# Two projections with the same weights as one: the high and low part of x side by side in a two-layer decoder trunk

## The chip, the cores and the metric

One core of a Trainium2 chip runs the whole program. The metric is the device time of one execution in microseconds (us), the median of the runs; lower is better. TensorE (PE) multiplies, ScalarE (ACT) and VectorE (DVE) do the elementwise work, SyncE (SP) issues the DMAs. TensorE writes its sums to PSUM, a small memory of eight banks of 128 partitions x 512 float32.

## What is computed

The reference takes 256 tokens of width 2048 through two layers. Cut to what matters here:

```python
def _even_layer(x, w_in, ...):
    hproj = x @ w_in                                  # 2048 -> 7704 columns
    (qa, kc, vc, ks, vs, kw, vw, ga, gate_a, qb, kb, vb, gate_b) = _split(hproj, EVEN_SIZES)
    o_a = _nsa(...) * jax.nn.silu(gate_a)             # sparse attention, 8 heads
    o_b = _stick_breaking(...) * jax.nn.silu(gate_b)  # 8 heads
    y = jnp.concatenate([o_a, o_b], axis=-1) @ w_out
    return _layer_norm(DEEPNORM_ALPHA * x + y, ln_g, ln_b)

def _odd_layer(x, w_in, ...):
    q, k, v, gate = _split(x @ w_in, ODD_SIZES)       # 2048 -> 8192 columns
    o = _diff_attn(q, k, v, ...) * jax.nn.silu(gate)  # 8 heads
    return _layer_norm(DEEPNORM_ALPHA * x + o @ w_out, ln_g, ln_b)
```

All of it is float32. Most of the arithmetic is the four big products with weight matrices.

## The kernel before

**Products in parts.** Every float32 operand of a big product is split into a high and a low part (`split`, L125: ACT casts the source to the high part, DVE subtracts it from the source to get the low one). A product a x b is then three matmuls: high x high, high x low, low x high, summed in PSUM.

**Two kinds of projection.** In the first kind, `xs_group` and `xs_apart`, tokens are stationary and 390 or 512 weight columns move (L202 to L204). In the second, `ws_block` (L176), 128 weight columns are stationary and the 256 tokens move, so that the result comes out transposed, [128 columns, 256 tokens]. A block covers the 2048 inputs in 16 steps k of 128, with three matmuls of 256 moving columns in each: weights high x tokens high (L181), weights high x tokens low (L182), weights low x tokens high (L183). `ws_pair` (L185) runs two blocks, one into each half of one PSUM bank, and hands the bank to the consumer. The query, key and gate columns of both layers go this way: kc, kr, qa, qb, kb, gate in the even layer, q and k in the odd one.

**Weights.** `load_split` brings a block's weights by one DMA (1 MB) to a tile `wr` (3 buffers) and splits it in two halves, each to a tile `wh` (high) and `wl` (low), 4 buffers each; a half holds 8 of the 16 steps.

**Moving operand.** `new_lhs` (L245) gives the tokens' high parts in four tiles and the low parts in four more; `lhs_of` picks the slice of step k. These tiles are xT (input), oT and oT1 (attention outputs), yT (the normalised rows between the layers).

**Attention.** Attention is written as generators. `tick` (L167) advances up to two of them after each block, so attention work of TensorE lies between and inside the projection blocks. The consumers of a pair are `rope` (DVE, four instructions), scaled copies (ACT) or `silu` (ACT and DVE).

**Order.** A scheduler orders the instructions of each engine when the program is built, by priorities (the program order) and its own estimates; buffers of a pool come free when their last reader is done. On the chip each engine takes its instructions in that order, each waiting for its semaphores. Names used below: `ss` are attention scores in PSUM, `sm` the softmax rows made of them, `pT` transposed probabilities in PSUM and `pk` their parts, `pcT` the same of the compressed branch, `aT` and `po` those of the odd layer's attention and its output, `yt` the transposes that become yT.

Of the kernel before, what the change touches and what calls it, by code (L numbers as in the profile page):

```python
# [10 lines left out]
F32 = mybir.dt.float32  # L11
F32R = mybir.dt.float32r
# [20 lines left out]
# columns of ev_w_in: q kc vc ks vs kw vw gates gate_a qb kb vb gate_b  # L33
# [3 lines left out]
# stationary-weight column blocks of the even layer, in the order they are used  # L37
# [3 lines left out]
# packed constants: name -> (offset, width)  # L41
# [42 lines left out]
def hybrid_trunk(ctx: ExitStack, tc: tile.TileContext, a):  # L84
# [10 lines left out]
    # the one table set with all of Exp, Ln, Abs, Square, Copy and Identity  # L95
# [21 lines left out]
    # ---- zeros through the tensor engine while the first loads are under way, so that its clock is up  # L117
# [6 lines left out]
    # ---- splitting float32 into two parts of 12 bits each, exactly  # L124
# [4 lines left out]
    def mm3(o, lhs, rhs, start, stop):  # L129
        """o += lhs.T @ rhs, both in parts"""  # L130
        (ah, al), (bh, bl) = lhs, rhs
        nc.tensor.matmul(o, ah, bh, start=start, stop=False, skip_group_check=True)
        nc.tensor.matmul(o, ah, bl, start=False, stop=False, skip_group_check=True)
        nc.tensor.matmul(o, al, bh, start=False, stop=stop, skip_group_check=True)

    # ---- weights: one DMA per tile, then the two parts
# [9 lines left out]
    def load_split(src, n, alloc=part, pieces=None, m=1):  # L146
        """pieces(j): called before each part of a half, which is then loaded and split by itself"""
        raw = raw_tile(n)
        if not pieces:
            nc.sync.dma_start(raw, src)  # L150
        out = []
        for s in range(2):
            h, l = alloc("wh", n // 2), alloc("wl", n // 2)
            w = n // 2 // m
            for j in range(m):
                d = slice((m * s + j) * w, (m * s + j + 1) * w)
                if pieces:
                    pieces(m * s + j)
                    nc.sync.dma_start(raw[:, d], src[:, d])
                split(h[:, j * w:(j + 1) * w], l[:, j * w:(j + 1) * w], raw[:, d])  # L160
            out.append((h, l))
        return out

    # work in stages, one stage of each after every block of a projection
# [11 lines left out]
    def ws_block(src, ps, xh, xl):  # L176
        """ps[cols, tokens] = W[:, 128 cols].T @ x.T"""
        parts = load_split(src.rearrange("p k c -> p (k c)"), 2048)
        for k in range(NK):
            h, l = (t.rearrange("p (k c) -> p k c", c=P)[:, k % 8, :] for t in parts[k // 8])  # L180
            nc.tensor.matmul(ps, h, xh(k), start=(k == 0), stop=False)  # L181
            nc.tensor.matmul(ps, h, xl(k), start=False, stop=False)  # L182
            nc.tensor.matmul(ps, l, xh(k), start=False, stop=(k == NK - 1))  # L183

    def ws_pair(src, i, name, xh, xl):  # L185
        ps = acc(name)
        for c in range(2):
            ws_block(src[i + c], ps[:, c * SEQ:(c + 1) * SEQ], xh, xl)
            tick()
        return ps.rearrange("p (c t) -> p c t", c=2)  # L190
# [4 lines left out]
    def xs_mm(o, t, parts, half, k0, w, xh, xl, start, stop, c0=0):  # L195
        """o[tokens of t, cols] += x[:, two k] @ W[two k, cols]"""
        h, l = (p.rearrange("p (k c) -> p k c", c=w) for p in parts[half])
        s = slice(t * P, (t + 1) * P)
        cs = slice(c0, c0 + o.shape[1])
        for j in range(2):  # L200
            k = k0 + 2 * half + j
            nc.tensor.matmul(o, xh(k)[:, s], h[:, j, cs], start=(start and j == 0), stop=False)  # L202
            nc.tensor.matmul(o, xh(k)[:, s], l[:, j, cs], start=False, stop=False)  # L203
            nc.tensor.matmul(o, xl(k)[:, s], h[:, j, cs], start=False, stop=(stop and j == 1))  # L204

    def xs_group(src, w, name, xh, xl, ahead=None):
        """ps[t][tokens, cols] = x @ W[:, w cols]"""
        ps = [acc(f"{name}{t}") for t in range(NT)]
        for kc in range(4):
            m = 2 if ahead and kc < 1 else 1  # L210
            parts = xs_parts(src, w, kc, part, ahead and (lambda j: ahead(kc, j * 2 // m, 2 // m)), m)
            order = [(half, t) for half in range(2) for t in range(NT)]
            if not ahead:
                order.sort(key=lambda z: z[1])
            for half, t in order:
                xs_mm(ps[t][:, :w], t, parts, half, 4 * kc, w, xh, xl, kc + half == 0, kc + half == 4)
            tick()
        return ps

    def xs_apart(src, name, xh, xl, in_units, orders, ready, n_last=1, m=1):  # L220
        """like xs_group, one token tile after the other, the weights kept; ready(t, c0, ps) after each"""
# [14 lines left out]
    # ---- constants  # L236
# [7 lines left out]
    # ---- x transposed, in parts  # L244
    def new_lhs(name):  # L245
        return ([unit(f"{name}h{i}", [4, SEQ], F32R) for i in range(4)],
                [unit(f"{name}l{i}", [4, SEQ], F32R) for i in range(4)])

    def lhs_of(parts):
        return [lambda k, t=t: t[k // 4][:, k % 4, :] for t in parts]  # L250

    xT = new_lhs("xT")
    xh, xl = lhs_of(xT)

    xraw = [unit("xraw", [4, SEQ]) for _ in range(4)]

    def load_x(i, k, n):
        xr = xraw[i][:, k:k + n]
        nc.sync.dma_start(xr, a["xT"][:, 4 * i + k:4 * i + k + n, :])
        split(xT[0][i][:, k:k + n], xT[1][i][:, k:k + n], xr)  # L260
# [15 lines left out]
    def load_constants():  # L276
        nc.sync.dma_start(cst, a["cst"])
        nc.sync.dma_start(sml, a["sml"])
        # lambda = exp(lq1.lk1) - exp(lq2.lk2) + lambda_init, negated, on every partition
# [11 lines left out]
    # ---- helpers  # L291
    def rope(ps, cos, sin, out):
        """ps, out: [128 d, 2, 256 tokens]"""
# [8 lines left out]
    def log_sigmoid_parts(g, w, tag):  # L302
        """e = ln(1 + exp(-|g|))"""
# [18 lines left out]
    def rsqrt(out, v, n, name):  # L322
        """out = v ** -0.5, one Newton step after exp(-ln(v) / 2)"""
# [9 lines left out]
    def softmax_rows(ps, n, mask, name):  # L333
        """ps: [128 q, 2, n] negated scaled scores -> unnormalised p and 1/sum for both."""
# [11 lines left out]
    def transposed(p, t, ps):  # L346
        """p: [128 q, (t+1)*128 keys] of query tile t into ps[keys, 3*128]: k0 t0 | k0 t1 | k1 t1"""
# [4 lines left out]
    def add_pv(o, v, pT, start, stop):  # L352
        """o[d, 256 q] += v.T @ p.T over both key tiles"""
# [3 lines left out]
    # =========================== even layer ===========================  # L357
    ws, xs = a["ev_ws"], a["ev_xs"]
    # token-major columns: gates | vs | vw | vb
# [25 lines left out]
    kvT = unit("kvT", [2, 2, SEQ])  # compressed-branch k, v: [d, (k v), head, token]  # L385
    for i in range(2):
        ps = ws_pair(ws, 2 * i, f"kc{i}", xh, xl)
        nc.scalar.copy(kvT[:, i], ps)
    kr = [unit(f"kr{i}", [2, 2, SEQ], F32R) for i in range(2)]  # roped keys: [d, head, (select window), token]
    for i in range(2):  # L390
        ps = ws_pair(ws, 4 + 2 * i, f"kr{i}", xh, xl)
# [4 lines left out]
    # compression MLPs  # L396
    kcmpT = cpool.tile([P, 2, NCMP], F32, name="kcmpT")
    # compressed values: their three products of parts in one pass, the parts at rows 0, 32 and 64
# [64 lines left out]
    # native sparse attention, two heads at a time  # L463
# [3 lines left out]
    def held(i):  # L467
        """for the attention of heads 2i and 2i+1 of all 16"""
# [4 lines left out]
    def nsa_proj(i):  # L473
        ps = ws_pair(ws, 8 + 2 * i, f"qa{i}", xh, xl)
# [8 lines left out]
    def nsa_attn(i, qc, qs):  # L483
# [3 lines left out]
        # compressed branch  # L487
# [20 lines left out]
        # selected and window branches  # L508
# [32 lines left out]
        pk0 = [unit(f"pk0{j}", [2, 2, SEQ], F32R) for j in range(2)]  # [key, (select window), head, query]  # L541
# [19 lines left out]
    def sb_proj(i):  # L561
        ps = ws_pair(ws, 16 + 2 * i, f"qb{i}", xh, xl)
        qb = wk("qc", [2, SEQ])
        nc.scalar.activation(qb, ps, AF.Copy, scale=SCALE)
        ps = ws_pair(ws, 24 + 2 * i, f"kb{i}", xh, xl)
# [49 lines left out]
    def gate_pair(i):  # L615
        """o = attention * silu(gate), in parts, for heads 2i and 2i+1 of all 16"""
        ps = ws_pair(ws, 32 + 2 * i, f"gate{i}", xh, xl)
        s = silu(ps.rearrange("p c t -> p (c t)"), 512)
        sl = slice(2 * (i % 2), 2 * (i % 2) + 2)
        nc.vector.tensor_mul(s, s, held(i).rearrange("p c t -> p (c t)"))  # L620
        split(oT[0][i // 2][:, sl].rearrange("p c t -> p (c t)"), oT[1][i // 2][:, sl].rearrange("p c t -> p (c t)"), s)
# [16 lines left out]
    def cols(halves, c):  # L638
        """columns c * 512 ... of a row of 2048 kept in two units"""
        return halves[c // 2][:, c % 2 * 512:(c % 2 + 1) * 512]  # L640

    # ---- output projection, residual and layer norm
# [9 lines left out]
    def out_layer(wout, lhs, resid, name, finish, g=None, n_last=1):  # L652
        """resid[t] = alpha * resid[t] + lhs @ wout (times g), then finish(t, its mean and 1 / deviation)"""
# [47 lines left out]
    def normalise(t, scale, bias):  # L701
        """resid[t] becomes the normalised row, its scaled and shifted transpose goes to yT"""
# [5 lines left out]
        for c in range(4):  # L708
# [8 lines left out]
            split(yT[0][c][:, :, ts], yT[1][c][:, :, ts], y)  # L717
# [4 lines left out]
    # =========================== odd layer ===========================  # L722
    yh, yl = lhs_of(yT)
    ws, xs = a["od_ws"], a["od_xs"]
# [20 lines left out]
    def diff_proj(h):  # L745
        ps = ws_pair(ws, 4 * h, f"q{h}", yh, yl)
        q = wk("qr", [2, SEQ])
        rope(ps, C("cosq"), C("sinq"), q)
        ps = ws_pair(ws, 4 * h + 2, f"k{h}", yh, yl)
# [66 lines left out]
    def gate_out(g, sg):  # L816
        yield
        for j in range(2):
# [5 lines left out]
            for b in range(2):  # L824
                c = 2 * j + b
                gs = gn1[:, 4 * g + c:4 * g + c + 1]
                nc.scalar.activation(oT[0][g][:, c], pt[:, b], AF.Copy, scale=gs)
                nc.vector.scalar_tensor_tensor(oT[1][g][:, c], pt[:, b], gs, oT[0][g][:, c].bitcast(F32),
# [8 lines left out]
    def store(t, scale, bias):  # L837
        """resid[t] is r * g: r * g * scale + (g * bias + b)"""
# [28 lines left out]
def _layout(x, ev_w_in, ev_pe_k, ev_pe_v, ev_w1_k, ev_w2_k, ev_w1_v, ev_w2_v, ev_w_out, ev_ln_g, ev_ln_b,  # L867
# [3 lines left out]
    def grouped(w, width):  # L871
        """[2048, n * width] -> [n, 128, 16, width]"""
# [54 lines left out]
```

## Time and profile before

| | us |
|---|---|
| median of 3 runs (977.92 to 978.41) | 978.25 |
| span of the profiled execution, first to last instruction | 976.2 |
| TensorE matmul busy | 966.6 |
| TensorE weight load busy | 891.6 |
| VectorE busy | 668.7 |
| ScalarE busy | 505.6 |

The profiled execution's own time is not listed apart from the three runs; its span lies 2.05 us under their median. Busy time is the union of an engine's instructions; matmuls overlap in it, since each is shown from its start to its modelled end while the next has begun. How densely TensorE works is therefore read from the distance between the starts of neighbouring matmuls, the pitch, and not from the length of one.

### The profile page before, as it was taken

What the parts mean: (1) busy time and instruction counts of PE and PEld (TensorE: products, weight loads), DVE (VectorE), ACT (ScalarE), POOL (GpSimd) and SP (SyncE); (2) the same over time, 40 slices, a digit from 0 to 9 for tenths busy, and PEclk for the clock granted to TensorE, in tenths of its full rate; (3) what the DMA queues carried; (4) which work ended last, traced back from release to release, by engine and by line L of the source; (5) the groups of instructions that cost most, each with busy time, mean ns of one, the idle gap of its engine ahead of it and who ended that gap; (6) DMA issues with size and microseconds to landing.
All of it is one profiled execution on the core that took longest, in us unless ns stands there. A gap on an engine that the chain in (4) does not pass through costs nothing.

```text
span 976.2 us, 15916 instructions
## 1 busy us (share of the span) xinstructions
PE 966.6 (99%) x6497; PEld 891.6 (91%) x6497; DVE 668.7 (69%) x1107; ACT 505.6 (52%) x812; POOL 1.2 (0%) x8
## 2 busy tenths in 40 slices
PE   8999999999999999999999999999999999999998
PEld 6999999999999999988888889999999988888886
DVE  6544577695766856666598556777778776667676
ACT  5544444475657856535473443455545556664340
POOL 0000000000000000000000000000000000000000
PEclk9999999999999999999999999999999999999999
DMA  8765546643334345756547555544544445557542
GB/s 306 256 207 195 186 169 249 257 138 121 136 123 141 130 174 177 277 193 229 180 150 266 207 176 178 189 156 170 173 167 154 160 168 177 191 193 258 194 151 87
DMA packets 30457, 180.80 MB, mean 185 GB/s; under 512 B 3504, under 2 KB 5296, under 8 KB 11952
## 3 DMA queue, kind: packets, MB, share of 16 engines
q1 hardware_dynamic: 30384, 179.79, 52.3%
q8 instruction: 51, 0.84, 0.3%
q14 instruction: 22, 0.18, 0.1%
HBM read 177.68 MB, written 2.10 MB: 184 GB/s over the span
## 4 chain that ended last, share of the span: by engine, by line
PE 96%; DMA 1%; DVE 1%; ACT 1%; SPq 0%; issue 0%; DVEq 0%; ACTq 0%
PE k L182 3%; PE k L183 3%; PE k L181 3%; PE gate L183 3%; PE q L182 3%; PE gate L182 3%; PE gate L181 3%; PE q L181 3%; PE q L183 3%; PE oo L204 3%; PE oo L202 3%; PE oo L203 3%; PE odv L203 3%; PE odg L202 3%; PE odv L202 3%; PE odg L203 3%
## 5 line engine op out<-in xcount | busy, mean ns | idle before, releaser
L127 DVE TENSOR_TENSOR wl<-wr,wh 128x1024 fp32r<-128x1024 f32 (+3 forms) x330 | 383.2, 1166 | 225.1 <-ACT wh L126 217.9
L126 ACT CAST wh<-wr 128x1024 fp32r<-128x1024 f32 (+3 forms) x330 | 329.7, 1003 | 349.6 <-PE eo L204 40.9
L181 PE MATMUL q<-yTh,wh 128*128 128x256 f32 x256 | 72.9, 285 | 0.0
L181 PE MATMUL gate<-xTh,wh 128*128 128x256 f32 x256 | 72.8, 284 | 0.0
L183 PE MATMUL gate<-xTh,wl 128*128 128x256 f32 x256 | 72.5, 283 | 0.0
L181 PE MATMUL k<-yTh,wh 128*128 128x256 f32 x256 | 72.4, 283 | 0.0
L182 PE MATMUL k<-yTl,wh 128*128 128x256 f32 x256 | 72.4, 283 | 0.0
L183 PE MATMUL k<-yTh,wl 128*128 128x256 f32 x256 | 72.4, 283 | 0.0
L182 PE MATMUL gate<-xTl,wh 128*128 128x256 f32 x256 | 72.4, 283 | 0.0
L183 PE MATMUL q<-yTh,wl 128*128 128x256 f32 x256 | 72.4, 283 | 0.0
L182 PE MATMUL q<-yTl,wh 128*128 128x256 f32 x256 | 72.4, 283 | 0.0
L204 PE MATMUL oo<-wh,oT1l 128*128 128x512 f32 (+1 forms) x144 | 52.7, 366 | 0.0
L203 PE MATMUL oo<-wl,oT1h 128*128 128x512 f32 (+1 forms) x144 | 52.7, 366 | 0.0
L202 PE MATMUL oo<-wh,oT1h 128*128 128x512 f32 (+1 forms) x144 | 52.7, 366 | 0.0
L202 PE MATMUL odg<-wh,yTh 128*128 128x512 f32 x128 | 50.3, 393 | 0.0
L202 PE MATMUL odv<-wh,yTh 128*128 128x512 f32 x128 | 50.1, 392 | 0.0
L202 PE MATMUL eo<-wh,oTh 128*128 128x512 f32 x128 | 50.0, 391 | 0.0
L203 PE MATMUL odv<-wl,yTh 128*128 128x512 f32 x128 | 50.0, 390 | 0.0
L204 PE MATMUL odv<-wh,yTl 128*128 128x512 f32 x128 | 49.9, 390 | 0.0
L203 PE MATMUL eo<-wl,oTh 128*128 128x512 f32 x128 | 49.9, 390 | 0.0
L204 PE MATMUL odg<-wh,yTl 128*128 128x512 f32 x128 | 49.9, 390 | 0.0
L203 PE MATMUL odg<-wl,yTh 128*128 128x512 f32 x128 | 49.8, 389 | 0.0
(287 smaller groups left out, 2494.0 us busy)
## 6 DMA issues: line engine op xcount, KB each, us to landing
wr<-in_ev_ws_dram SPq DMA_DIRECT2D x48, 1024.0 KB, 4.8
wr<-in_od_xs_dram SPq DMA_DIRECT2D x32, 1024.0 KB, 4.8
wr<-in_od_ws_dram SPq DMA_DIRECT2D x32, 1024.0 KB, 4.9
wr<-in_ev_wo_dram SPq DMA_DIRECT2D x16, 1024.0 KB, 4.8
wr<-in_od_wo_dram SPq DMA_DIRECT2D x16, 1024.0 KB, 4.9
wr<-in_ev_xs_dram SPq DMA_DIRECT2D x12, 780.0 KB, 4.6
w<-in_w_dram SPq DMA_DIRECT2D x8, 512.0 KB, 8.4
wr<-in_ev_xs_dram SPq DMA_DIRECT2D x6, 390.0 KB, 6.7
```

The costliest lines, as they stand in the source:

```text
L126: nc.scalar.copy(h, src)
L127: nc.vector.tensor_sub(l, src, h.bitcast(F32))
L181: nc.tensor.matmul(ps, h, xh(k), start=(k == 0), stop=False)
L182: nc.tensor.matmul(ps, h, xl(k), start=False, stop=False)
L183: nc.tensor.matmul(ps, l, xh(k), start=False, stop=(k == NK - 1))
L202: nc.tensor.matmul(o, xh(k)[:, s], h[:, j, cs], start=(start and j == 0), stop=False)
L203: nc.tensor.matmul(o, xh(k)[:, s], l[:, j, cs], start=False, stop=False)
L204: nc.tensor.matmul(o, xl(k)[:, s], h[:, j, cs], start=False, stop=(stop and j == 1))
```

## The change

The tokens' high and low parts now lie side by side: `new_lhs` gives eight tiles of two steps each, and in each step 256 columns of the high part are followed by 256 of the low part. `ws_block` issues one matmul of 512 moving columns with the high weights, into a whole PSUM bank, and one of 256 with the low weights, onto its first half. So each block has a bank of its own, and the two halves have to be added: ACT copies the second half to a tile `wsum`, DVE adds the first half to it. The consumers read `wsum` in place of PSUM. The products in `xs_group` and `xs_apart` are as before, on slices of the new tiles. Where a split writes four steps, as for yT, it is now two splits of two steps. Comments and docstrings are dropped.

```diff
-    def ws_block(src, ps, xh, xl):
+    def ws_block(src, ps, xx):
         parts = load_split(src.rearrange("p k c -> p (k c)"), 2048)
         for k in range(NK):
             h, l = (t.rearrange("p (k c) -> p k c", c=P)[:, k % 8, :] for t in parts[k // 8])
-            nc.tensor.matmul(ps, h, xh(k), start=(k == 0), stop=False)
-            nc.tensor.matmul(ps, h, xl(k), start=False, stop=False)
-            nc.tensor.matmul(ps, l, xh(k), start=False, stop=(k == NK - 1))
-
-    def ws_pair(src, i, name, xh, xl):
-        ps = acc(name)
+            nc.tensor.matmul(ps, h, xx(k), start=(k == 0), stop=False, skip_group_check=True)
+            nc.tensor.matmul(ps[:, :SEQ], l, xx(k)[:, :SEQ], start=False, stop=(k == NK - 1), skip_group_check=True)
+
+    def ws_pair(src, i, name, xx):
+        out = wk("wsum", [2, SEQ])
         for c in range(2):
-            ws_block(src[i + c], ps[:, c * SEQ:(c + 1) * SEQ], xh, xl)
+            ps = acc(f"{name}{c}")
+            ws_block(src[i + c], ps, xx)
+            nc.scalar.copy(out[:, c], ps[:, SEQ:])
+            nc.vector.tensor_add(out[:, c], out[:, c], ps[:, :SEQ])
             tick()
-        return ps.rearrange("p (c t) -> p c t", c=2)
+        return out
...
     def new_lhs(name):
-        return ([unit(f"{name}h{i}", [4, SEQ], F32R) for i in range(4)],
-                [unit(f"{name}l{i}", [4, SEQ], F32R) for i in range(4)])
+        return [unit(f"{name}{i}", [2, 2, SEQ], F32R) for i in range(8)]
 
     def lhs_of(parts):
-        return [lambda k, t=t: t[k // 4][:, k % 4, :] for t in parts]
+        return [lambda k, j=j: parts[k // 2][:, k % 2, j, :] for j in range(2)]
+
+    def both_of(parts):
+        return lambda k: parts[k // 2][:, k % 2].rearrange("p j t -> p (j t)")
+
+    def two(parts, j, i):
+        return parts[i][:, :, j, :]
...
-            split(yT[0][c][:, :, ts], yT[1][c][:, :, ts], y)
+            for j in range(2):
+                split(two(yT, 0, 2 * c + j)[:, :, ts], two(yT, 1, 2 * c + j)[:, :, ts], y[:, 2 * j:2 * j + 2])
```

**TensorE, odd layer, key projection of head 1**, the end of its first block and the start of its second. Before (`k1` is the pair's PSUM bank, `yTh3`, `yTl3` the high and low tokens of the last four steps):

```order
L181 MATMUL k1_6333<-yTh3_4609,wh_6340 128x256
L182 MATMUL k1_6333<-yTl3_4613,wh_6340 128x256
L183 MATMUL k1_6333<-yTh3_4609,wl_6341 128x256
L181 MATMUL k1_6333<-yTh0_4606,wh_6394 128x256
L182 MATMUL k1_6333<-yTl0_4610,wh_6394 128x256
L183 MATMUL k1_6333<-yTh0_4606,wl_6395 128x256
```

Now, with a bank for each block (`k10`, `k11`):

```order
L181 MATMUL k10_5648<-yT7_3989,wh_5655 128x512
L182 MATMUL k10_5648<-yT7_3989,wl_5656 128x256
L181 MATMUL k11_5693<-yT0_3982,wh_5696 128x512
L182 MATMUL k11_5693<-yT0_3982,wl_5697 128x256
L181 MATMUL k11_5693<-yT1_3983,wh_5696 128x512
```

Three instructions of 256 columns have become one of 512 and one of 256; what stands next to them has not moved.

**ScalarE, odd layer, around the end of head 1's key projection.** Before (`wh` are casts of weight halves, the numbers rise with the program; L795 squares the attention output for its mean):

```order
L126 CAST wh_6558<-wr_6556 128x1024
L126 CAST wh_6562<-wr_6556 128x1024
L126 CAST aTs0_6454<-aT_6450 128x384
L126 CAST wh_6654<-wr_6652 128x1024
L126 CAST q1_6468<-qr_6326 128x256
L126 CAST wh_6658<-wr_6652 128x1024
```

Now:

```order
L190 COPY wsum_5647<-k10_5648 128x256
L126 CAST wh_5834<-wr_5832 128x1024
L126 CAST wh_5838<-wr_5832 128x1024
L190 COPY wsum_5647<-k11_5693 128x256
L126 CAST aTs0_5742<-aT_5738 128x384
L126 CAST wh_5917<-wr_5915 128x1024
L126 CAST wh_5921<-wr_5915 128x1024
L126 CAST ks_5753<-qc_5746 128x512
```

A copy of each block's second half stands between the casts: that of block k10 ahead of wh_5834, which belongs to the second block after k11, and that of k11 two casts later.

**VectorE, even layer, where the attention of three head pairs meets** (L338, after the change L352, named ISA, makes softmax rows `sm` of scores `ss`). Before, from the low parts of block kb1's weights on:

```order
L127 TENSOR_TENSOR wl_2489<-wr_2486,wh_2488 128x1024
L127 TENSOR_TENSOR wl_2493<-wr_2486,wh_2492 128x1024
L127 TENSOR_TENSOR pk01_2134<-pT0_2345,pk00_2133 128x2x256
L127 TENSOR_TENSOR pk11_2136<-pT1_2346,pk10_2135 128x2x128
L127 TENSOR_TENSOR pcT_1241<-tcmp_2357,pcT_1241 15x512
L127 TENSOR_TENSOR pk01_2366<-pT0_2369,pk00_2365 128x2x256
L127 TENSOR_TENSOR pk11_2368<-pT1_2370,pk10_2367 128x2x128
L338 ISA sm_2385,smst_2386<-ss_2381,cst_86 128x128
L338 ISA smst_2386 128x1
L338 ISA sm_2385,smst_2386<-ss_2381,cst_86 128x128
L338 ISA smst_2386 128x1
L338 ISA sm_2399,smst_2400<-ss_2395,cst_86 128x256
```

Now, up to the low part of the second weight half of block qb11:

```order
L127 TENSOR_TENSOR pcT_1137<-tcmp_2084,pcT_1137 15x512
L127 TENSOR_TENSOR pk01_2093<-pT0_2096,pk00_2092 128x2x256
L127 TENSOR_TENSOR pk11_2095<-pT1_2097,pk10_2094 128x2x128
L352 ISA sm_2112,smst_2113<-ss_2108,cst_86 128x128
L352 ISA smst_2113 128x1
L352 ISA sm_2112,smst_2113<-ss_2108,cst_86 128x128
L352 ISA smst_2113 128x1
L352 ISA sm_2126,smst_2127<-ss_2122,cst_86 128x256
L352 ISA smst_2127 128x1
L352 ISA sm_2126,smst_2127<-ss_2122,cst_86 128x256
L352 ISA smst_2127 128x1
L127 TENSOR_TENSOR wl_2144<-wr_2137,wh_2143 128x1024
```

Before, the weights of the next pair were split ahead of this attention work, which lies in the second block of qb1; now the second half of that same block's weights is split behind it. On TensorE, 2 matmuls of block qb11 and 10 of an attention output (`po`) stand between the scores ss_2122 and the first matmul that reads wl_2144.

## Rows read from the trace of the kernel before

**Rows 1.** The page: busy time of each engine, share of the span, instructions.
```profile
PE 966.6 (99%) x6497; PEld 891.6 (91%) x6497; DVE 668.7 (69%) x1107; ACT 505.6 (52%) x812; POOL 1.2 (0%) x8
```
**Rows 2.** The page: chain of work that ended last, shares by engine.
```profile
PE 96%; DMA 1%; DVE 1%; ACT 1%; SPq 0%; issue 0%; DVEq 0%; ACTq 0%
```
**Rows 3.** Waits of TensorE: total us, times, longest us.
```profile
PE ev L202 <- ACT wh L126: 2.0, 2, 1.2
...
PE cmp L425 <- DMA w<-in_w_dram: 0.7, 1, 0.7
```
**Rows 4.** Timeline, TensorE, odd layer: start us, length us, instruction; 256 columns.
```profile
604.60 0.28 PE L183 MATMUL k<-yTh,wl 128*128 128x256 f32 x1
...
606.04 0.28 PE L183 MATMUL q<-yTh,wl 128*128 128x256 f32 x1
```
**Rows 5.** Timeline, TensorE, odd layer, product with 512 moving columns.
```profile
549.64 0.39 PE L203 MATMUL odv<-wl,yTh 128*128 128x512 f32 x1
...
553.04 0.39 PE L203 MATMUL odv<-wl,yTh 128*128 128x512 f32 x1
```
**Rows 6.** Timeline, TensorE, attention output, where 512 and 256 columns alternate.
```profile
238.55 0.40 PE L134 MATMUL po<-pk,vsw 128*128 128x512 f32 x1
238.79 0.28 PE L132 MATMUL po<-pk,vsw 128*128 128x256 f32 x1
...
239.02 0.28 PE L134 MATMUL po<-pk,vsw 128*128 128x256 f32 x1
239.14 0.40 PE L132 MATMUL po<-pk,vsw 128*128 128x512 f32 x1
```
**Rows 7.** The page: DMA issues, count, KB each, us to landing.
```profile
wr<-in_ev_ws_dram SPq DMA_DIRECT2D x48, 1024.0 KB, 4.8
...
wr<-in_od_ws_dram SPq DMA_DIRECT2D x32, 1024.0 KB, 4.9
```
**Rows 8.** Groups by line and shape: busy us, mean ns, idle before.
```profile
L126 ACT CAST wh<-wr 128x1024 fp32r<-128x1024 f32 x280 | 293.1, 1049 | 316.5 <-PE q L182 40.1 <-PE k L182 36.1 <-PE odv L204 29.5
...
L126 ACT CAST q<-qr 128x256 fp32r<-128x256 f32 x8 | 3.2, 402 | 0.0
...
L126 ACT CAST pk<-pT 128x256 fp32r<-128x256 f32 x8 | 3.0, 374 | 0.9 <-PE pT L528 0.9
...
L127 DVE TENSOR_TENSOR wl<-wr,wh 128x1024 fp32r<-128x1024 f32 x280 | 341.5, 1224 | 200.0 <-ACT wh L126 193.7 <-PE pT L527 1.7
...
L127 DVE TENSOR_TENSOR yTl<-yt,yTh 128x512 fp32r<-128x512 f32 x8 | 5.5, 689 | 0.7 <-ACT yTh L126 0.5
...
L587 DVE TENSOR_TENSOR sbz<-sz,cst 128x256 f32<-128x256 f32 x4 | 1.7, 418 | 0.0
```
**Rows 9.** Timeline, ScalarE, odd layer, weight casts and what they waited for.
```profile
599.40 1.05 ACT L126 CAST wh<-wr 128x1024 fp32r<-128x1024 f32 x1 [1.83 <-PE k L182]
602.28 1.05 ACT L126 CAST wh<-wr 128x1024 fp32r<-128x1024 f32 x1 [1.83 <-PE k L182]
```
**Rows 10.** Stretches: length, busy us of PE, PEld, DVE, ACT, POOL, clock, DMA.
```profile
200.00:220.00 20.00, 19.96 (x159) 19.06 (x158) 18.47 (x69) 15.79 (x44) 0.00 (x0) 1.00 0.43 156
...
500.00:520.00 20.00, 20.00 (x98) 16.56 (x97) 19.38 (x38) 11.33 (x16) 0.00 (x0) 1.00 0.77 289
```
**Rows 11.** Timeline, TensorE, where plain float32 matmuls (`cmp`) interrupt a block.
```profile
158.37 0.28 PE L182 MATMUL qa<-xTl,wh 128*128 128x256 f32 x1
158.58 0.64 PE L425 MATMUL cmp<-w,blk 128*30 128x128 f32 x16
159.16 0.38 PE L183 MATMUL qa<-xTh,wl 128*128 128x256 f32 x1
159.38 0.28 PE L181 MATMUL qa<-xTh,wh 128*128 128x256 f32 x1
```
**Rows 12.** Timeline, VectorE, softmax rows behind scores in the attention stretch.
```profile
218.49 0.42 DVE L338 CUSTOM_DVE_ANT_0 sm<-ss,cst 128x256 f32<-128x256 f32 x1 [0.19 <-PE ss L134]
218.84 0.08 DVE L338 DVE_READ_ACCUMULATOR2_ANT smst<- 128x1 f32 x1
218.84 0.42 DVE L338 CUSTOM_DVE_ANT_0 sm<-ss,cst 128x256 f32<-128x256 f32 x1
```
**Rows 13.** Timeline, ScalarE, between the layers: rows of token tile 1 normalised.
```profile
500.15 1.53 ACT L705 ACTIVATE x<-x,mv 128x512 f32<-128x512 f32 x2 [0.20 <-DVE mv L676]
```
**Rows 14.** Timeline, TensorE, between the layers: first transposes of token tile 1.
```profile
501.34 0.60 PE L712 MATMUL yt<-cst,x 128*128 128x128 f32 x4
```

More of the change, by code (lines that the diff above doesn't have):

```diff
@@ L245, in new_lhs @@
     def new_lhs(name):
[L246 to L247 removed]
+        return [unit(f"{name}{i}", [2, 2, SEQ], F32R) for i in range(8)]
     def lhs_of(parts):
[L250 removed]
+        return [lambda k, j=j: parts[k // 2][:, k % 2, j, :] for j in range(2)]
[3 more added lines that the diff above has]
+        return parts[i][:, :, j, :]
     xT = new_lhs("xT")
     xh, xl = lhs_of(xT)
+    xx = both_of(xT)
     xraw = [unit("xraw", [4, SEQ]) for _ in range(4)]
@@ L259, in load_x @@
         nc.sync.dma_start(xr, a["xT"][:, 4 * i + k:4 * i + k + n, :])
-        split(xT[0][i][:, k:k + n], xT[1][i][:, k:k + n], xr)
+        m = min(n, 2)
+        for j in range(0, n, m):
+            u, b = divmod(4 * i + k + j, 2)
+            split(two(xT, 0, u)[:, b:b + m], two(xT, 1, u)[:, b:b + m], xr[:, j:j + m])
     first = xs_group(a["ev_xs"][0], EV_XS_W, "ev0_", xh, xl, load_x)
@@ L386, in hybrid_trunk @@
     for i in range(2):
-        ps = ws_pair(ws, 2 * i, f"kc{i}", xh, xl)
+        ps = ws_pair(ws, 2 * i, f"kc{i}", xx)
         nc.scalar.copy(kvT[:, i], ps)
@@ L390, in hybrid_trunk @@
     for i in range(2):
-        ps = ws_pair(ws, 4 + 2 * i, f"kr{i}", xh, xl)
+        ps = ws_pair(ws, 4 + 2 * i, f"kr{i}", xx)
         k = wk("kr", [2, SEQ])
@@ L473, in nsa_proj @@
     def nsa_proj(i):
-        ps = ws_pair(ws, 8 + 2 * i, f"qa{i}", xh, xl)
+        ps = ws_pair(ws, 8 + 2 * i, f"qa{i}", xx)
         qc = wk("qc", [2, SEQ])
@@ L561, in sb_proj @@
     def sb_proj(i):
-        ps = ws_pair(ws, 16 + 2 * i, f"qb{i}", xh, xl)
+        ps = ws_pair(ws, 16 + 2 * i, f"qb{i}", xx)
         qb = wk("qc", [2, SEQ])
         nc.scalar.activation(qb, ps, AF.Copy, scale=SCALE)
-        ps = ws_pair(ws, 24 + 2 * i, f"kb{i}", xh, xl)
+        ps = ws_pair(ws, 24 + 2 * i, f"kb{i}", xx)
         kb = wk("qr", [2, SEQ])
@@ L615, in gate_pair @@
     def gate_pair(i):
-        ps = ws_pair(ws, 32 + 2 * i, f"gate{i}", xh, xl)
+        ps = ws_pair(ws, 32 + 2 * i, f"gate{i}", xx)
         s = silu(ps.rearrange("p c t -> p (c t)"), 512)
-        sl = slice(2 * (i % 2), 2 * (i % 2) + 2)
         nc.vector.tensor_mul(s, s, held(i).rearrange("p c t -> p (c t)"))
-        split(oT[0][i // 2][:, sl].rearrange("p c t -> p (c t)"), oT[1][i // 2][:, sl].rearrange("p c t -> p (c t)"), s)
+        split(two(oT, 0, i), two(oT, 1, i), s.rearrange("p (c t) -> p c t", c=2))
     steps = [(nsa_proj, nsa_attn, i) for i in range(4)] + [(sb_proj, sb_attn, i) for i in range(4)]
@@ L723, in hybrid_trunk @@
     yh, yl = lhs_of(yT)
+    yy = both_of(yT)
     ws, xs = a["od_ws"], a["od_xs"]
@@ L745, in diff_proj @@
     def diff_proj(h):
-        ps = ws_pair(ws, 4 * h, f"q{h}", yh, yl)
+        ps = ws_pair(ws, 4 * h, f"q{h}", yy)
         q = wk("qr", [2, SEQ])
         rope(ps, C("cosq"), C("sinq"), q)
-        ps = ws_pair(ws, 4 * h + 2, f"k{h}", yh, yl)
+        ps = ws_pair(ws, 4 * h + 2, f"k{h}", yy)
         k = wk("qc", [2, SEQ])
@@ L826, in gate_out @@
                 gs = gn1[:, 4 * g + c:4 * g + c + 1]
-                nc.scalar.activation(oT[0][g][:, c], pt[:, b], AF.Copy, scale=gs)
-                nc.vector.scalar_tensor_tensor(oT[1][g][:, c], pt[:, b], gs, oT[0][g][:, c].bitcast(F32),
+                h, l = (two(oT, z, 2 * g + j)[:, b] for z in range(2))
+                nc.scalar.activation(h, pt[:, b], AF.Copy, scale=gs)
+                nc.vector.scalar_tensor_tensor(l, pt[:, b], gs, h.bitcast(F32),
                                                op0=ALU.mult, op1=ALU.subtract)
```

## The prediction

> **What bounds the kernel now.** I read the page first: TensorE is busy for 966.6 of 976.2 us, and the chain that ended last is TensorE for 96% [rows 1, 2]. The list of its waits holds few: two weight casts at the start for 2.0 us and one DMA of compression weights for 0.7 are the largest [rows 3]. So TensorE sets the time, and a change is worth what it takes out of TensorE's own stream, less any new wait. A matmul's length in the list is no price, because neighbours overlap; the price is the distance between starts. In the second kind of projection twelve steps take 606.04 - 604.60 = 1.44 us, 0.1200 us each for 256 columns [rows 4]. In the products with 512 columns fifteen steps take 553.04 - 549.64 = 3.40 us, 0.2267 us each [rows 5]. The clock was granted in full in the stretches read (1.00, the 2.4 GHz level) [rows 10]. Twice the columns cost 0.1067 us more, so a matmul is 0.1067 us per 256 columns plus 0.0133 us that does not grow with them.
>
> **The change, part by part.**
>
> *Matmuls.* There are 48 + 32 = 80 blocks [rows 7] with 16 steps each, 1280 steps. A step was 3 x 0.1200 = 0.3600 us and becomes 0.2267 + 0.1200 = 0.3467 us: the columns are the same 768, and one fixed part is gone. 1280 x 0.0133 = **17.1 us** off the path, 0.213 us per block. The trace of before has no stream that alternates the two widths in every step. The nearest is the attention output, where a 256 follows a 512 after 0.24 us and a 512 follows a 256 after 0.12 [rows 6], rounded to hundredths; read like that a step would be 0.36 and the gain nothing, so the bounds are 0 and 17.1. More is excluded, as no long run has a 256 sooner than 0.1200. I take 17.1, because the runs of twelve and fifteen steps carry more digits than a single pair does.
>
> The Trainium skill ("TensorE: Matmul & The Clock Gate", section "Back-to-back issue gap") gives N / 2.4 ns plus 2.5 ns at the full clock, a fixed part five times smaller than the one in these rows. By that the removed instructions would give 1280 x 0.0025 = 3.2 us, an estimate from that page of the Trainium skill, and the time would be about 977. The two runs of starts decide against it here.
>
> *Copy and add.* Each block gets an ACT copy of 128 x 256 from PSUM (0.374 by the nearest such copy, at most 0.402) and a DVE add of PSUM and SBUF (0.418 by the masked scores, the same operands) [rows 8]. 80 x 0.374 = 29.9 us make ACT about 536 of 961 us; 80 x 0.418 = 33.4 make DVE about 702. Off TensorE's path I cost them at nothing. What hides them is the lead of the weight splits: a cast starts when TensorE has freed a buffer of four, every 2.88 us, after waiting 1.83 us for it [rows 9], so the half it makes is used three halves later, 3 x 2.88 - 1.05 = 7.6 us after the cast ends. The copy waits for its block's last matmul, and what is queued behind it on ACT is the cast for a half about two blocks on, with SP's next weight DMA behind the subtraction on DVE. The delay is 0.37 us against that lead. Without the cover each block would end in copy, cast and subtraction, 0.374 + 1.049 + 1.224 = 2.65 us [rows 8]. The consumers get their sum 0.8 us later (copy and add); the scores of the odd layer stand two blocks behind their keys, about 11 us, so nobody waits. The bank of a block is free three blocks before it is needed again.
>
> *yT in two splits.* Eight splits of 512 columns become sixteen of 256: on DVE 2 x 0.418 - 0.689 = 0.147 us more for each [rows 8], 1.2 us in all, in the stretch where DVE has no idle time (19.38 of 20 us) [rows 10]. Half of it, 0.59, lies ahead of the statistics of token tile 1, whose normalisation begins on ACT at 500.15 (two quarters in 1.53 us) [rows 13], while TensorE takes the first quarter at 501.34 [rows 14], about 0.4 us after it is done. So some 0.2 us of wait there and as much again for tile 1's own splits: 0 to 1.2, I take 0.5.
>
> *Order of attention work.* The scheduler's order interrupts the blocks' stream with plain float32 matmuls 66 times in place of 62. An interruption puts starts apart by 0.21 and 0.22 where 0.12 is usual [rows 11], about 0.2 in all: 4 x 0.2 = 0.8 (bounds 0 and 1.5, if some are twice as dear).
>
> *The weights behind the attention.* In block qb11 the second weight half's low part is now split behind softmax rows that need scores of the same block. From the scores' end DVE needs 0.35 + 0.35 for two rows [rows 12] and 1.224 for the split [rows 8], plus 0.2 to start [rows 12]: 2.1 us. TensorE has until then 2 matmuls of the block and 10 of an output, 7 of 512 and 5 of 256 columns, about 2.2 us by the pitches above. That is a tie in a stretch where DVE was busy for 18.47 of 20 us [rows 10]; I take 0.4, between 0 and 3 (one split late, twice).
>
> *The DMA of the compression weights* took TensorE 0.7 us [rows 3]. TensorE comes to it sooner while the transfer takes as long: 1.5 blocks x 0.213 = 0.3 us more (0 to 0.6).
>
> **Sum**, against the profiled execution's span: 976.2 - 17.1 + 0.5 + 0.8 + 0.4 + 0.3 = 961.1. The median of the runs lies 2.05 us above that span, so the forecast is **963.1 us**.
>
> **The rivals.**
>
> *The fixed part stays.* The 0.0133 us might belong to the columns or to something that the longer matmul keeps, as the hundredths of the mixed pairs allow [rows 6]. Then TensorE's stream is as long as before and only the additions are left: 978.25 + 2.0 = 980.2, and anything between that and 963.1 if a part stays. Against it: the same 0.0133 fits both widths [rows 4, 5]. The Trainium skill's 2.5 ns is of this kind, with the 977 above.
>
> *The attention stretch chokes.* DVE is nearly full from 200 to 220 us [rows 10] and gets an add in every block; if the late split meets a backlog, TensorE waits some 3 us in two or three places between 200 and 260 us: 961.1 + 7 + 2.05, about 970. Against it: elsewhere the splits keep their lead, and only one pair's weights lost it.
>
> *Slower: the copies hold up the weights.* ACT takes its queue in order. If the casts behind the copies ran only at a block's end, TensorE would wait for copy and cast in each, 1.42 us against the 0.213 saved: 978 + 80 x (1.42 - 0.21) = 1075. It decides from 0.213 us of wait per block. For it: a copy now stands between the casts of nearby blocks. Against it: the cast behind a copy is for a half about two blocks later, and the lead of 7.6 us is far above 0.37 [rows 9].
>
> **How the numbers follow.** I give the forecast 0.84, the fixed part that stays 0.06 (half of it ending within 0.2% of before or a little faster, half slower by 2 us), the choke 0.06, the held-up weights 0.04. The range takes the bounds of the terms: without any additions 961.2, and 0.7 less if today's DMA wait goes; with each at its upper end 961.2 + 1.2 + 1.5 + 3 + 0.6 = 967.5. So 960.5 to 967.5; rivals that lie outside hold 0.16. About 0.2%, or 2 us, is what a measurement of this kernel can tell from no change. Faster by more than that: 0.84 + 0.06 and a little of the first rival, 0.92; within it 0.02; slower 0.06.
>
> **What would show it.** In the changed kernel's timeline a step of a block should take 0.347 us and a half of weights 2.77 us (0.36 and 2.88: the fixed part stayed). TensorE's waits should name the same two or three causes, with less than 2 us added around qb11, the transposes between the layers and the compression weights. ACT and DVE should gain 80 instructions each at about 0.37 and 0.42 us, with casts still waiting for TensorE and not TensorE for casts. A wait of TensorE on `wh` or `wl` in the odd layer would prove me wrong, as would a pitch of 0.24 us for the wide matmul.

## The result and the profile after

The changed kernel takes **966.1 us** (median, 965.0 to 966.4) against 978.26: 0.9874 of the time before, interval 0.986 to 0.9888, so 12.2 us or 1.3% faster. The forecast was 963.1 with a range of 960.5 to 967.5. The profiled execution has a span of 963.2 us (before: 976.2); its own time is 965.02, the fastest of the four.

The page's row of engines answers [rows 1]. Its columns are busy us, share of the span, instructions:

```profile
PE 956.5 (99%) x5217; PEld 821.1 (85%) x5217; DVE 693.0 (72%) x1195; ACT 529.6 (55%) x900; POOL 1.2 (0%) x8
```

TensorE has 1280 instructions fewer (6497 to 5217), ACT and DVE 88 more each: 80 copies and adds, and 8 more from the splits of `yT`. TensorE is still the bound. TensorE's waits answer [rows 3] (us in total, times, longest):

```profile
PE idle L122 <- DVE eps L705: 1.2, 1, 1.2
PE ev L205 <- ACT wh L126: 0.4, 1, 0.4
PE ev L205 <- ACT xT L126: 0.3, 1, 0.3
PE u L864 <- DVE diag L862: 0.2, 1, 0.2
```

None of these waits stands in a block: the list names neither a block's weights nor the compression weights `w`, nor the layer transition. It is even 2.4 us shorter than before, 0.7 of it the wait for `w`, the rest at the start of the program.

So the stream itself has to be read. The next fence has TensorE's timeline in the gate blocks of the even layer: two narrow matmuls sixteen steps apart.

```profile
351.98 0.27 PE L182 MATMUL gate<-xT,wl 128*128 128x256 f32 x1
...
357.52 0.27 PE L182 MATMUL gate<-xT,wl 128*128 128x256 f32 x1
```

5.54 us for sixteen steps, 0.346 us a step: the pitch that was forecast, 0.3467. The same in the odd layer's keys, where [rows 4] were read:

```profile
590.14 0.28 PE L182 MATMUL k<-yT,wl 128*128 128x256 f32 x1
590.49 0.28 PE L182 MATMUL k<-yT,wl 128*128 128x256 f32 x1
590.84 0.28 PE L182 MATMUL k<-yT,wl 128*128 128x256 f32 x1
591.20 0.28 PE L182 MATMUL k<-yT,wl 128*128 128x256 f32 x1
...
595.79 0.28 PE L182 MATMUL k<-yT,wl 128*128 128x256 f32 x1
```

Here sixteen steps take 5.65 us, 0.353 a step, half-way between the forecast and the old 0.360. The instructions are the same, nobody is waited for, and the granted clock is 1.00 in both places (columns as in [rows 10]):

```profile
350.00:395.00 45.00, 45.00 (x262) 39.36 (x261) 32.13 (x40) 30.48 (x45) 0.00 (x0) 1.00 0.56 195
...
590.00:640.00 50.00, 50.00 (x296) 43.86 (x295) 40.95 (x80) 27.91 (x56) 0.00 (x0) 1.00 0.51 179
```

**The stream of alternating widths has two rhythms.** The trace's starts, which have nanoseconds, show them (wide to narrow + narrow to wide, step by step):

```
fast   231+112  233+117  231+113  232+118  ...     or 230+117 in every step    346.7 ns a step
slow   233+117  241+120  236+113, and again        a cycle of three steps      353.3 ns a step
before 120+120+120                                                             360.0 ns a step
```

A rhythm holds until another kind of matmul interrupts the stream: the first thirteen blocks of the even layer are slow from end to end, the last nine gate blocks are fast, most of the odd layer is slow. Of 1280 steps 1240 are neither interrupted nor waiting; together they lie 5.5 us above 0.3467 each, which is two thirds of them in the slow rhythm.

The casts of ACT at the same place answer [rows 9] (in brackets: idle before it, and what ended it):

```profile
590.34 1.05 ACT L126 CAST wh<-wr 128x1024 fp32r<-128x1024 f32 x1 [1.77 <-PE k L181]
591.29 0.37 ACT L190 COPY wsum<-k 128x256 f32<-128x256 f32 x1
593.16 1.05 ACT L126 CAST wh<-wr 128x1024 fp32r<-128x1024 f32 x1 [1.50 <-PE k L181]
595.99 1.05 ACT L126 CAST wh<-wr 128x1024 fp32r<-128x1024 f32 x1 [1.78 <-PE k L181]
```

The copy stands in a gap in which ACT had waited for TensorE, and the next cast still waits 1.50 us for TensorE. A half of weights takes 2.82 or 2.83 us: 2.88 before, 2.77 forecast. The groups by shape answer [rows 8] (busy us, mean ns):

```profile
L127 DVE TENSOR_TENSOR yT<-yt,yT 128x256 fp32r<-128x256 f32 x16 | 6.6, 420 | 0.7 <-ACT yT L126 0.7
...
L190 ACT COPY wsum<-k 128x256 f32<-128x256 f32 x16 | 5.8, 364 | 0.0
...
L191 DVE TENSOR_TENSOR wsum<-wsum,k 128x256 f32<-128x256 f32 x16 | 6.6, 415 | 0.0
```

### The profile page after: what moved, and what is told of

Its sections match the earlier page's. It is cut to its first block, busy times and chain, and to the rows that moved or that the text cites. A ratio compares the mean times of both kernels' runs of the same rounds, so it can differ in the third digit from the quotient of the medians.

```text
span 963.2 us, 13548 instructions
## 1 busy us (share of the span) xinstructions
PE 956.5 (99%) x5217; PEld 821.1 (85%) x5217; DVE 693.0 (72%) x1195; ACT 529.6 (55%) x900; POOL 1.2 (0%) x8
## 4 chain that ended last, share of the span: by engine, by line
PE 97%; issue 1%; DMA 1%; ACT 0%; SPq 0%; DVE 0%; DVEq 0%
PE k L181 6%; PE q L181 6%; PE gate L181 6%; PE k L182 3%; PE q L182 3%; PE gate L182 3%; PE qb L181 3%; PE odv L206 3%; PE oo L206 3%; PE oo L205 3%; PE kb L181 3%; PE oo L207 3%; PE odv L207 3%; PE odg L206 3%; PE eo L205 3%; PE odv L205 3%
## 5 line engine op out<-in xcount | busy, mean ns | idle before, releaser
L181 PE MATMUL q<-yT,wh 128*128 128x512 f32 x256 | 91.0, 399 | 0.0
L181 PE MATMUL k<-yT,wh 128*128 128x512 f32 x256 | 90.8, 399 | 0.0
L181 PE MATMUL gate<-xT,wh 128*128 128x512 f32 x256 | 89.9, 396 | 0.0
L182 PE MATMUL k<-yT,wl 128*128 128x256 f32 x256 | 71.9, 281 | 0.0
L182 PE MATMUL q<-yT,wl 128*128 128x256 f32 x256 | 71.6, 280 | 0.0
L182 PE MATMUL gate<-xT,wl 128*128 128x256 f32 x256 | 71.2, 278 | 0.0
L207 PE MATMUL oo<-wh,oT 128*128 128x512 f32 (+1 forms) x144 | 52.8, 366 | 0.0
L205 PE MATMUL oo<-wh,oT 128*128 128x512 f32 (+1 forms) x144 | 52.7, 366 | 0.0
L206 PE MATMUL oo<-wl,oT 128*128 128x512 f32 (+1 forms) x144 | 52.7, 366 | 0.0
L205 PE MATMUL odg<-wh,yT 128*128 128x512 f32 x128 | 50.3, 393 | 0.0
L205 PE MATMUL odv<-wh,yT 128*128 128x512 f32 x128 | 50.0, 392 | 0.0
L207 PE MATMUL odv<-wh,yT 128*128 128x512 f32 x128 | 50.0, 390 | 0.0
L207 PE MATMUL odg<-wh,yT 128*128 128x512 f32 x128 | 49.9, 390 | 0.0
```

Source lines behind the costliest of these rows:

```text
L181: nc.tensor.matmul(ps, h, xx(k), start=(k == 0), stop=False, skip_group_check=True)
L182: nc.tensor.matmul(ps[:, :SEQ], l, xx(k)[:, :SEQ], start=False, stop=(k == NK - 1), skip_group_check=True)
```

## The experiments

After the result two theories stood. **Theory 1**: the missing 3 us are in the rhythm of TensorE's stream, which comes from the alternation of 512 and 256 columns. **Theory 2**: the new copies and adds, which read PSUM beside TensorE, disturb its stream. Each run is compared with runs of the kernel before that were taken alongside it (977.5 to 978.0 us).

### Runs of one width, eight and two

The order within a block, in place of wide, narrow, wide, narrow (the first run takes `n = 8`, the second `n = 2`):

```diff
-        for k in range(NK):
-            nc.tensor.matmul(ps, h, xx(k), ...)
-            nc.tensor.matmul(ps[:, :SEQ], l, xx(k)[:, :SEQ], ...)
+        for k0 in range(0, NK, n):
+            for k in range(k0, k0 + n):
+                nc.tensor.matmul(ps, h(k), xx(k), ...)
+            for k in range(k0, k0 + n):
+                nc.tensor.matmul(ps[:, :SEQ], l(k), xx(k)[:, :SEQ], ...)
```

> The changed kernel, with the matmuls of a half in another order: its eight of 512 columns first, then its eight of 256, in place of 512, 256, 512, 256. Same instructions, same sums. Theory 1, the alternation of widths has a slow rhythm: a step takes 0.3467 us in every block, the 5.5 us that the steps of the changed kernel lie above that are gone, median 966.1 - 5.5 = 960.6 us, and the runs lie as close together as those of the kernel before (0.5 us). Theory 2, the copies and adds disturb TensorE's stream: nothing changes, 966.1 us.

> The same with groups of two: 512, 512, 256, 256. Theory 1 in the form 'each change of width costs': half as many changes, half of the 5.5 us is left, 963.3 us. Theory 1 in the form 'only strict alternation falls into the slow rhythm': 960.6 us as with groups of eight. Theory 2: 966.1 us.

Measured: 962.78 us with eight (0.9841 of before, 0.9827 to 0.9854) and **962.16 us** with two (0.9837, 0.9824 to 0.9851). By the medians they are 14.8 and 15.4 us below the kernel before, where the changed kernel was 12.2 below: about 3 us faster, with the same instructions, copies and adds. That speaks for theory 1, but the 960.6 were not reached, and two did not lie half-way. The timeline with eight shows why (start, length, instruction, how many):

```profile
594.99 2.00 PE L182 MATMUL q<-yT,wh 128*128 128x512 f32 x8
596.83 1.12 PE L184 MATMUL q<-yT,wl 128*128 128x256 f32 x8
597.78 2.00 PE L182 MATMUL q<-yT,wh 128*128 128x512 f32 x8
```

Eight wide ones take 1.84 us from start to start, 230 ns each and not the 226.7 of the long products [rows 5]; the eight narrow ones 0.95. In nanoseconds a run of wide ones behind narrow ones goes 233, 236, 228, 233, 231, 226, 227, 227: five of them until the pitch is even, and the first narrow one has 113 in place of 120. Net, each return from narrow to wide costs 20 ns. A block has two and takes 5.587 us; with runs of two it takes 5.573:

```profile
595.30 0.63 PE L182 MATMUL q<-yT,wh 128*128 128x512 f32 x2
595.77 0.39 PE L184 MATMUL q<-yT,wl 128*128 128x256 f32 x2
596.00 0.62 PE L182 MATMUL q<-yT,wh 128*128 128x512 f32 x2
596.46 0.40 PE L184 MATMUL q<-yT,wl 128*128 128x256 f32 x2
596.69 0.63 PE L182 MATMUL q<-yT,wh 128*128 128x512 f32 x2
```

Two steps take 0.70 and 0.69 us in turn. This is a steady rhythm of its own, the same in 46 of 68 uninterrupted blocks to one nanosecond.

### All additions without the merge

The wide matmul taken apart again, everything else as changed. In the first of the two runs all sixteen steps of a block were taken apart; there each half of a bank starts its own sum within the same step, and a part of the sums is lost by this (the output has a relative error of 0.58), though every instruction runs. The second leaves the first step wide and computes everything.

```diff
-            nc.tensor.matmul(ps, h, xx(k), ...)
+            nc.tensor.matmul(ps[:, :SEQ], h, xx(k)[:, :SEQ], ...)
+            nc.tensor.matmul(ps[:, SEQ:], h, xx(k)[:, SEQ:], ...)
```

> The changed kernel with the wide matmul taken apart again: two of 256 columns into the two halves of the bank, everything else (layout of the tokens, a bank for each block, copy and add, yT in two splits) as changed. Prices all additions together. The prediction put them at 0.5 + 0.8 + 0.4 + 0.3 = 2.0 us: 980.3 us. Theory 1 with the traces (products behind the transposes between the layers 0.45 us longer, TensorE's named waits 2 us shorter): 978.3 to 978.8 us, steps at 0.3600 us throughout. Theory 2: the copies and adds cost 5.5 us here too, about 983.8 us.

> The changed kernel with the wide matmul taken apart in fifteen of a block's sixteen steps (the first stays wide, since it also starts the sums of both halves). All additions are there, and 80 of the 1280 saved instructions: 17.07 / 16 = 1.1 us of the gain. By the prediction's 2.0 us of additions: 978.3 + 2.0 - 1.1 = 979.2 us, or by the kernel before of the last call 978.4. By the run that took all sixteen apart (0.4 us above the kernel before): 0.7 us below the kernel before of the same call.

Measured: 977.96 us beside 977.58 of before (ratio 0.9992 to 1.0009), and 976.73 beside 977.95 (0.9975 to 0.9993). The first puts the additions at 0.4 us (-0.8 to 0.9), the second at -1.2 + 1.1 = -0.1 (-1.4 to 0.4). Theory 2 would need 5.5 in both and falls. The forecast's 2.0 us is too much.

### Copy and add twice

```diff
+            again = wk("again", [SEQ])
+            nc.scalar.copy(again, ps[:, SEQ:])
+            nc.vector.tensor_add(again, again, ps[:, :SEQ])
```

> The changed kernel with copy and add of every block done twice, the second time into a tile that nobody reads. Theory 1: hidden like the first ones, 966.1 us, at most 1 us more. Theory 2: what the copies and adds cost is doubled, 966.1 + 5.5 = 971.6 us. The prediction's rival of held-up weights: more than that, with TensorE waiting for weight casts.

Measured: 970.08 us (0.9916, 0.9901 to 0.993), 7.5 us below before where the changed kernel was 12.2 below. That is 4 to 5 us more. My expectation of at most 1 missed, and the time alone would fit theory 2. But theory 2 needs a stream that is slower everywhere, and TensorE's waits say otherwise (those that the changed kernel does not have):

```profile
PE kb L181 <- DVE again L194: 1.0, 1, 1.0
PE pTb L367 <- ACT sbz L612: 0.8, 2, 0.6
...
PE cmpt L460 <- DVE cmph L456: 0.4, 1, 0.4
PE kb L182 <- DVE wl L127: 0.3, 1, 0.3
```

2.5 us, all in the attention stretch of the even layer: a block's first matmul waits for a bank that DVE has not emptied, and a weight half and attention operands come late. TensorE's busy time from 190 to 270 us falls from 79.88 us in the changed kernel to this (columns as in [rows 10]):

```profile
190.00:270.00 80.00, 78.29 (x470) 66.72 (x469) 66.33 (x214) 56.26 (x141) 0.00 (x0) 1.00 0.35 120
```

Another 1.2 us is rhythm: the uninterrupted steps lie 6.7 us above 0.3467, not 5.5, because the gate blocks came out slow. About 1 us of the even layer's blocks is put down to nothing here. So the forecast's rival of the choking attention stretch is near: one more copy and add per block brings waits close to the place that it named, though the longest of them is for a bank (at 194 us) and only 0.3 us is for a weight half (at 223 us), the cause that it named.

### Other run lengths

> The changed kernel with six orders of a block's matmuls in turn, two blocks each: runs of 1 (as changed), 2, 4, 8 and 16 of one width, and 8 wide, 8 narrow, 8 narrow, 8 wide. Only the times of whole, uninterrupted blocks count, not the kernel's. So far a block takes 5.650 or 5.547 us with runs of 1, 5.573 with runs of 2, 5.587 with runs of 8. Theory 1a, every change from narrow to wide costs some ns more until the stream is even again, about 20 ns after long runs: 4 gives between 5.57 and 5.63, 16 gives 5.567, the mirrored order 5.567. Theory 1b, the excess belongs to a lasting rhythm that is set where the stream is entered: the order within the block does not decide it, and blocks of every order come in two kinds 0.10 us apart.

> In every block 8 wide and 8 narrow in the first half of the weights, 8 narrow and 8 wide in the second: one change from narrow to wide per block. Theory 1a: 5.567 us a block, 80 x 0.020 = 1.6 us less than groups of eight, 961.2 us by the figures of that call. Theory 1b: like the groups of eight, 962.8 us. The low parts of the second half are needed 1.8 us sooner; if the lead of the splits is too short somewhere, 1 to 3 us more.

> Runs of four of one width. Theory 1a: four changes from narrow to wide per block at 3 to 20 ns, 5.56 to 5.63 us a block, 961.5 to 966 us. Theory 1b: 962.5 us like groups of two and eight.

> The changed kernel once more, with a second profile. If the two rhythms are set by chance where the stream is entered, other blocks are slow than in the first profile, and the runs lie 1 us and more apart; if the program sets them, the same blocks are slow. Either way 965 to 966.5 us, with about 50 of the 80 blocks slow.

The kernel with six orders in turn (one execution, 963.38 us) gives a block's length for each, the others confirm them. The blocks are whole and uninterrupted, from the trace's starts; blocks that lose about 0.1 us in their first step, behind other work, are left out:

```
matmuls of one width in a row   returns to wide   block us                 above 5.547, ns   ns per return
1, fast rhythm                  16                5.546 to 5.556           0                 0
1, slow rhythm                  16                5.640 to 5.665           107               6.7
2                                8                5.573                    26                3.3
4                                4                5.613                    66                16.6
8                                2                5.587                    40                20
8, second half mirrored          1                5.567 (5.595)            20 (48)           20
16                               1                5.566 to 5.571 (5.540)   20 (-7)           20
```

The slow rhythm's excess is that of its mean, 5.653. The mirrored value in parentheses belongs to blocks behind an interruption or behind a block that ended on narrow matmuls, so that they start with a second return. The value in parentheses for sixteen belongs to two blocks behind a mirrored one, which ends on wide matmuls, so that they have no return. Runs of eight and sixteen and the mirrored order obey theory 1a, 20 ns for each return to the wide matmul. Runs of four pay 16.6 ns for each of four returns, within the bounds that theory 1a gave, and are the dearest of the groups. Theory 1b falls: but for runs of one, the order does decide a block's time. The kernel with fours:

```profile
596.45 1.09 PE L196 MATMUL q<-yT,wh 128*128 128x512 f32 x4
597.38 0.64 PE L196 MATMUL q<-yT,wl 128*128 128x256 f32 x4
597.85 1.09 PE L196 MATMUL q<-yT,wh 128*128 128x512 f32 x4
```

1.40 us for four steps, 0.350 each. Whole kernels follow the blocks: 964.66 us with fours (0.9867), 962.85 mirrored (0.985). The mirrored order was expected 1.6 us ahead of the eights and is not. The queries and keys of the odd layer take as long as with the eights, to 0.1 us, since 20 of their 32 blocks stand behind an interruption, and one wait of 0.6 us for `sbz` stands in the even layer's attention that the eights do not have.

The changed kernel once more: 965.84 us (965.5 to 965.9; 0.988). 65 of 68 uninterrupted blocks have the rhythm that they had in the first profile; three blocks of the attention stretch that were fast are now slow, 0.1 us each. So the program sets the rhythm in all but a few blocks; that chance takes part where a block's entry shifts by some nanoseconds from execution to execution is likely, but not shown.

### What sets the rhythm

> The changed kernel with six orders in turn, two blocks each, that begin otherwise and then alternate as the change does: a run of 2 wide and 2 narrow ahead, of 3 and 3, of 4 and 4, of 8 and 8; eight steps alternating and then narrow ahead of wide in each step; eight steps alternating and then runs of 2. Only the steps within uninterrupted blocks count. The rhythm is set where the stream is entered: behind one and the same run, all alternating steps come out at one and the same pitch, 0.3467 or 0.3533 us, in every block with that order. The rival: the pitch of the alternating steps hangs on what came ahead of the block and not on the run, or it falls back to 0.3533 by itself after some steps.

In this kernel (one execution, 965.34 us) four of the six orders give a block a run in front and then alternate. Two neighbouring gate blocks with four wide and four narrow in front, the narrow matmuls of the run, the first narrow one of the alternating part and a later one:

```profile
352.19 0.63 PE L198 MATMUL gate<-xT,wl 128*128 128x256 f32 x4
352.89 0.28 PE L198 MATMUL gate<-xT,wl 128*128 128x256 f32 x1
...
356.70 0.28 PE L198 MATMUL gate<-xT,wl 128*128 128x256 f32 x1
...
357.75 0.64 PE L198 MATMUL gate<-xT,wl 128*128 128x256 f32 x4
358.46 0.28 PE L198 MATMUL gate<-xT,wl 128*128 128x256 f32 x1
...
362.00 0.28 PE L198 MATMUL gate<-xT,wl 128*128 128x256 f32 x1
```

Eleven steps in 3.81 us (0.346) in the first block, ten in 3.54 (0.354) in the second: the same order, the same tokens `xT`, the two rhythms. Counted over the uninterrupted blocks, two in front gave 4 fast and 8 slow, three 5 and 6, four 6 and 6, eight 0 and 12. So a short run in front does not decide it alone. The rhythm of the block ahead matters: where a block with three or four in front followed another without a break, it was slow behind a fast one in six cases of six, and fast behind a slow one in five of seven. Behind eight wide and eight narrow in front the slow rhythm came every time. In none of them, and nowhere in the two profiles of the changed kernel, did an alternating stretch change its rhythm by itself. My first form of the expectation (one run, one rhythm) holds for eight alone; its rival holds for the rest.

## Why the prediction was right, and by what it was off

**Right**: faster, in the range, 12.2 us of 15.2 forecast. TensorE's instructions were the bound, the fixed part of each is on the path, and the added work on ACT and DVE is not. What the fixed part belongs to is not shown: each matmul has a load of weights of its own (6497 of both before, 5217 now), so the merge took out 1280 of either. The copies measured 361 to 366 ns for the 374 forecast, the adds 412 to 416 for 418, and the casts kept waiting for TensorE. The rival of held-up weights did not come.

**The term that was mis-sized is the first**: 1280 steps at 0.3467 us. The step took the pitch of long runs of one width, 120.0 and 226.7 ns [rows 4, 5], and added them. In the slow rhythm, two thirds of the steps, 233 to 241 ns behind the wide matmul and 113 to 120 behind the narrow one come to 0.3533. With the 5.5 us of the rhythm the term is 11.6 and not 17.1. One sign that the prediction had named against itself, a pitch of 0.24 us for the wide matmul, is there in every third step of the slow rhythm (241 ns).

The prediction had rows of a mixed stream in hand, the attention output [rows 6], and misread them. The widths there do not alternate: three wide ones and three narrow ones stand in turn. And the 0.24 + 0.12 that it read as a step of 0.36 is rounding: in nanoseconds those two distances are 232 and 118. The whole stretch says it without nanoseconds, from its first start to the one behind its sixth pair:

```profile
238.08 0.40 PE L132 MATMUL po<-pk,vsw 128*128 128x512 f32 x1
...
240.18 0.40 PE L557 MATMUL po<-pcT,vcmp 79*128 79x512 f32 x1
```

2.10 us for six wide and six narrow ones, 0.350 a pair. That would have put the term at 1280 x 0.010 = 12.8 us, close to the 11.6 measured. That a part of the 17.1 stays is the case that the first rival named in passing, "anything between that and 963.1 if a part stays", and its chance of 0.06 was too small: I took the bounds 0 and 17.1 from one rounded pair and from streams of one width, and then the upper bound as the value.

**The additions were too dear.** Their sum was 2.0; the two runs without the merge give about 0.1, and together with the rhythm that is the result: 978.26 - 17.1 + 5.5 + 0.1 = 966.8, with 966.1 measured. One by one:

- `yT` in two splits: forecast 0.5. From start to start the products of the odd layer's values are 0.40 to 0.45 us longer in both profiles of the changed kernel and in the two unmerged kernels. The size is right; the place is not the wait that I described, since no row names one. The gaps are under 0.12 us each.
- Interruptions of the blocks: forecast 0.8. From the first block's start to the last one's end, the products between the layers left out, TensorE took 12.0 us less than before. The steps with their rhythm account for 11.6 and the wait for `w` for 0.7, so that 0.3 us is left for the four interruptions more.
- The weights of block qb11 behind softmax rows: forecast 0.4. No wait stands there. DVE was busy for 18.22 of the 20 us, hardly less than before [rows 10], and the split came in time:

```profile
200.00:220.00 20.00, 20.00 (x122) 17.39 (x122) 18.22 (x70) 15.49 (x44) 0.00 (x0) 1.00 0.32 106
```

- The compression weights: forecast 0.3 more; the wait of 0.7 us was gone [rows 3]. The first of these matmuls came 7.4 us after the first issue of that transfer, 8.1 before, and found the data there. In the runs without the merge the wait was 1.3 and 0.3 us, so it varies by more than my term.

The sum for the profiled execution then closes: -1.2 - 17.1 + 5.5 + 0.45 + 0.3 - 0.7 - 0.3 = -13.05, with 13.0 between the spans. The 1.2 is the earlier start of the first block (75.64 us after the first instruction, 76.82 before), the last 0.3 the shorter end behind TensorE's last matmul. Neither was forecast. TensorE's waits at the start of the program were 2.4 us in the profile of before, 0.7 in this one, and 0.7 to 1.8 in the others, of merged and unmerged kernels alike. So up to 1 us of this profile's lead is luck, and the median does not have it. The prediction's list of the largest waits also left out one of 1.2 us, at the first matmuls of the program; it is 1.2 after the change too and bears on nothing.

The Trainium skill's fixed part ("TensorE: Matmul & The Clock Gate", section "Back-to-back issue gap"), which it gives for an isolated matmul and not for a stream that also loads weights, would have given 977 by estimate. The measured gain is four times its 3.2 us; where one width follows itself these traces show 13.3 ns, and where widths change another 0 or 6.7 ns a pair.

**What stays open** is what in TensorE makes the two rhythms (the matmuls, or the loads of weights between them), and why four in a row cost more than two or eight. The runs show that the order of the instructions and what came just ahead bear on it; the same tokens at the same place are read in both rhythms.

## What to carry to other kernels

Take the pitch of an instruction stream from rows with a like succession of shapes, and over a whole stretch of them: pitches of uniform runs need not add up in a mixed one, and a single pair is lost in the rounding. Here the uniform runs gave 0.3467 us a step, one pair 0.36 and a stretch of twelve 0.350; the mean of the uninterrupted steps is 0.351. When a merge leaves instructions of two sizes, try the order in which they stand as a change of its own: here it brought another 3 us on top of the merge's 12, with the same instructions (962.16 us with two of each in turn; eights and the mirrored order lie within 0.7 us of that, which the intervals do not tell apart). And price added work on the off-path engines by doubling it once: it tells how much of the cover is left and where it ends first.

## What the hardware showed unexpectedly

The same alternating stream of 512 and 256 columns runs at 346.7 or 353.3 ns a pair, at a granted clock of 1.00 both times, with a period of three pairs in the slow case, for almost 80 us at a stretch, until something interrupts it. Behind a run of narrow matmuls five wide ones take 233, 236, 228, 233 and 231 ns until they run at 227. In two executions of the changed kernel the rhythm is the same in 65 of 68 blocks.
